# One level of Strassen's product in 12 of 22 blocks of an up projection, and a later split of the activations

## Chip, core and metric

The kernel runs on one core of a Trainium2 chip. The metric is the time of one execution on the device in microseconds (us); before the change it is 1796.58 us, the median of 3 runs (1796.41 to 1797.27). TensorE (PE) multiplies matrices and adds into PSUM; VectorE (DVE), ScalarE (ACT) and GpSimd (POOL) do everything else; SyncE (SP) issues most transfers from DRAM. Each engine works through its own instructions in order, and semaphores join them.

## What is computed

Two layers on a sequence of 512 tokens of width 1024, in float32: normalization and modulation, a projection for three attention-like branches, their gated merge, and a feed-forward part. The change concerns the last:

```python
h2 = modulate(rms_norm(x, norm2_g), shift2, scale2)
u, g = jnp.split(h2 @ w_up, 2, axis=-1)      # w_up: 1024 x 5632, u and g 2816 wide
u = causal_dwconv(u, w_conv, b_conv)         # 3 taps along the tokens
y = (jax.nn.silu(u) * g) @ w_down            # 2816 x 1024
x = x + gate2[:, None, :] * y
```

## The kernel before

Tokens lie along the free dimension (512 columns), features on the 128 partitions. To keep the precision of float32, each operand is split into a high part in the TensorE format float32r and a low part, the rest; a product takes three matmuls (mm3, L239): high weights by high activations (L240), high weights by low activations (L241), low weights by high activations (L242).

The weights lie in DRAM in the order of their use, as 302 units of 128 x 1024 (eight blocks of 128 x 128). Three engines handle each unit: SP loads it into one of 4 buffers wr (L113 to L115), ACT casts it to wh (L123), DVE subtracts to get wl (L132). prep_to and dma_to (called by ahead) keep these steps some units ahead of TensorE; there are 5 buffers each of wh and wl. A column block (col_block) is one unit: 24 matmuls of 512 columns into one PSUM bank. What evacuates the bank is appended to a list (pend) and emitted by flush within the next block, so the order of the instructions on DVE and ACT is that in which Python emits them; nothing reorders them.

The feed-forward part has 22 blocks j, each a column block for u and one for g. head_group makes the first three of each while the norm is still being finished. Then j = 3 to 21 follow one by one. ff_evac makes the convolution and Silu from PSUM (ACT L959, DVE L960 and L962, ACT L964), multiplies by g (DVE L965) and splits the result into fah (ACT L468) and fal (DVE L469), which the down projection reads: for each of 8 output blocks, 22 x 3 matmuls of 512 columns. Sums for adaLN (one load ar and one DVE instruction, L152, each) run along in every second tick. The activations x (8 tiles) stay in SBUF throughout; 60 slots of 128 x 512 serve all other tiles.

## Time and profile before

| | |
|---|---|
| median of 3 runs | 1796.58 us |
| the profiled execution | 1795.69 us, its span 1793.9 us |
| mean granted TensorE clock | 0.999 |
| moved by DMA | 220.00 MB, mean 123 GB/s |
| wh, 302 casts on ACT | 314.4 us busy |
| wl, 302 subtractions on DVE | 368.7 us busy |
| matmuls of L240, L241, L242 on hhi and hlo | 3 x 1296 |

Rows of groups read: line, engine, operation, output and inputs by the program's names, shape and count, then the busy time and the mean duration of one in ns, then idle time before them and what ended it. Rows of the timeline read: start in us, duration in us, engine, line, operation, and in brackets the idle time before it and what ended it. Matmuls overlap in their rows, so their pace is the distance between starts. Rows of windows read: the stretch, its length, busy time and count for PE, weight loads, DVE, ACT and POOL, then the granted clock (1.00 is full), the busy share of the DMA engines and GB/s.

### The profile page before, as it was taken

What the parts mean: (1) busy time and instruction counts of PE and PEld (TensorE: products, weight loads), DVE (VectorE), ACT (ScalarE), POOL (GpSimd) and SP (SyncE); (2) the same over time, 40 slices, a digit from 0 to 9 for tenths busy, and PEclk for the clock granted to TensorE, in tenths of its full rate; (3) what the DMA queues carried; (4) which work ended last, traced back from release to release, by engine and by line L of the source; (5) the groups of instructions that cost most, each with busy time, mean ns of one, the idle gap of its engine ahead of it and who ended that gap; (6) DMA issues with size and microseconds to landing.
All of it is one profiled execution on the core that took longest, in us unless ns stands there. A gap on an engine that the chain in (4) does not pass through costs nothing.

```text
span 1793.9 us, 22042 instructions
## 1 busy us (share of the span) xinstructions
PE 1781.2 (99%) x8737; PEld 1485.9 (83%) x8737; DVE 999.0 (56%) x1499; ACT 675.3 (38%) x1125; POOL 88.7 (5%) x112
## 2 busy tenths in 40 slices
PE   8999999999999999999999999999999999999999
PEld 6888778888888888888898887888888988888887
DVE  7777654565666876664256576534335465444321
ACT  4674433432324433332137543334223244333220
POOL 3221100000000000000002010000000000000000
PEclk9999999999999999999999999999999999999999
DMA  9332233455533565554223322322322223232231
GB/s 347 122 128 71 71 100 113 140 177 176 187 130 106 188 224 197 189 188 144 80 71 126 110 71 71 117 83 71 103 97 82 73 94 129 94 101 99 70 123 43
DMA packets 64947, 220.00 MB, mean 123 GB/s; under 512 B 7320, under 2 KB 7746, under 8 KB 64844
## 3 DMA queue, kind: packets, MB, share of 16 engines
q1 hardware_dynamic: 64140, 216.47, 36.0%
q0 software_dynamic: 704, 2.11, 0.4%
q8 instruction: 69, 1.13, 0.3%
q14 instruction: 34, 0.28, 0.0%
HBM read 216.44 MB, written 2.11 MB: 122 GB/s over the span
## 4 chain that ended last, share of the span: by engine, by line
PE 96%; DVE 3%; ACT 1%; DMA 0%; issue 0%; SPq 0%; POOL 0%; ACTq 0%; DVEq 0%
PE bm L240 24%; PE bm L242 24%; PE bm L241 24%; PE bm L369 4%; PE ga L369 4%; PE bm L537 3%; PE bm L538 3%; PE bm L539 3%; PE fs L654 1%; PE fo L680 1%; PE go L766 0%; DVE wl L132 0%; PE ro L821 0%; PE rs L794 0%; PE oT L753 0%; PE fT L670 0%
## 5 line engine op out<-in xcount | busy, mean ns | idle before, releaser
L132 DVE TENSOR_TENSOR wl<-wr,wh 128x1024 fp32r<-128x1024 f32 x302 | 368.7, 1224 | 317.5 <-ACT wh L123 317.0
L240 PE MATMUL bm<-hhi,wh 128*128 128x512 f32 x1296 | 515.7, 398 | 0.0
L242 PE MATMUL bm<-hhi,wl 128*128 128x512 f32 x1296 | 505.1, 390 | 0.0
L241 PE MATMUL bm<-hlo,wh 128*128 128x512 f32 x1296 | 504.8, 389 | 0.0
L123 ACT CAST wh<-wr 128x1024 fp32r<-128x1024 f32 x302 | 314.4, 1047 | 290.6 <-PE bm L241 218.3
L240 PEld LDWEIGHTS bm<-hhi,wh 128*128 128x128 f32 x1296 | 243.4, 188 | 52.1 <-issue 2.8
L242 PEld LDWEIGHTS bm<-hhi,wl 128*128 128x128 f32 x1296 | 243.2, 188 | 51.7
L241 PEld LDWEIGHTS bm<-hlo,wh 128*128 128x128 f32 x1296 | 243.5, 188 | 51.1 <-issue 1.4
L240 PE MATMUL bm<-fah,wh 128*128 128x512 f32 (+1 forms) x374 | 140.9, 377 | 0.0
L241 PE MATMUL bm<-fal,wh 128*128 128x512 f32 (+1 forms) x374 | 140.8, 377 | 0.0
L242 PE MATMUL bm<-fah,wl 128*128 128x512 f32 (+1 forms) x374 | 140.8, 377 | 0.0
L152 DVE SCALAR_TENSOR_TENSOR ar<-ar,cact 128x1024 f32<-128x1024 f32 x80 | 97.4, 1218 | 0.0
L537 PE MATMUL bm<-wh,hhi 128*128 128x512 f32 (+1 forms) x256 | 96.9, 379 | 0.0
L538 PE MATMUL bm<-wl,hhi 128*128 128x512 f32 (+1 forms) x256 | 93.5, 365 | 0.0
L539 PE MATMUL bm<-wh,hlo 128*128 128x512 f32 (+1 forms) x256 | 93.3, 365 | 0.0
L927 DVE SCALAR_TENSOR_TENSOR x<-bm,mod,x 128x512 f32<-128x512 f32 (+1 forms) x39 | 25.5, 654 | 100.0 <-PE bm L242 99.9
L240 PEld LDWEIGHTS bm<-fah,wh 128*128 128x128 f32 x374 | 70.4, 188 | 12.9
L241 PEld LDWEIGHTS bm<-fal,wh 128*128 128x128 f32 x374 | 70.4, 188 | 12.9
L242 PEld LDWEIGHTS bm<-fah,wl 128*128 128x128 f32 x374 | 70.4, 188 | 12.9
L965 DVE TENSOR_TENSOR fu<-fu,bm 128x512 f32<-128x512 f32 x42 | 28.9, 688 | 69.9 <-PE bm L242 61.6
L964 ACT ACTIVATE fu<-fu 128x512 f32<-128x512 f32 x44 | 27.8, 632 | 94.2 <-DVE fu L962 94.2
L890 ACT ACTIVATE mg<-bm,der 128x512 f32<-128x512 f32 x48 | 32.9, 685 | 73.7 <-PE bm L242 73.7
(230 smaller groups left out, 2346.5 us busy)
## 6 DMA issues: line engine op xcount, KB each, us to landing
wr<-wall SPq DMA_DIRECT2D x302, 512.0 KB, 3.4
ar<-wada SPq DMA_DIRECT2D x80, 512.0 KB, 3.3
ad<-wada SPq DMA_DIRECT2D x32, 256.0 KB, 6.3
x<-xT SPq DMA_DIRECT2D x8, 256.0 KB, 4.7
cumb<-cumd POOLq DMA_DIRECT2D x8, 256.0 KB, 4.7
dec<-tabs SPq DMA_DIRECT2D x8, 256.0 KB, 4.1
out<-x SPq DMA_DIRECT2D x8, 256.0 KB, 2.1
cos<-tabs SPq DMA_DIRECT2D x2, 256.0 KB
```

Source lines behind the costliest of these rows:

```text
L123: A.copy(hi, raw[i])
L132: V.tensor_tensor(lo, raw.pop(i), hi.bitcast(F32), op=ALU.subtract)
L152: V.scalar_tensor_tensor(out=r, in0=r, scalar=1.0, in1=cact, op0=ALU.mult, op1=ALU.mult, accum_out=mod[l][:, b:b + 1])
L240: T.matmul(o, lhsT=wh, rhs=ah, start=first, stop=False)
L241: T.matmul(o, lhsT=wh, rhs=al, start=False, stop=False)
L242: T.matmul(o, lhsT=wl, rhs=ah, start=False, stop=last)
L369: T.matmul(banks[f % GB][:, ts], lhsT=got[f // 8][wi][:, (f % 8) * 128:(f % 8) * 128 + 128], rhs=h[kc][hi][:, ts], start=kc == 0 and hf != ...
L537: T.matmul(o, lhsT=h[k][0][:, bs], rhs=wh[:, ws], start=k == 0, stop=False)
L538: T.matmul(o, lhsT=h[k][0][:, bs], rhs=wl[:, ws], start=False, stop=False)
L539: T.matmul(o, lhsT=h[k][1][:, bs], rhs=wh[:, ws], start=False, stop=k == KD - 1)
L890: A.activation(g, o, AF.Tanh, scale=0.5, bias=der[l][:, i * 8 + j:i * 8 + j + 1])
L965: V.tensor_tensor(t, t, pg, op=ALU.mult)
```

## The change

The last 12 blocks of each layer (j = 10 to 21) are made in three groups of four. In a group, the weights form a 2 x 2 matrix of halves: u and g by the first and second half of the 1024 inputs; the activations one of input halves by token halves. Seven products of halves take the place of eight. Each is 48 matmuls of 256 columns, in two units (the 14 of a group are called u0 to u13), and products that belong to one sum add up in PSUM or are added on evacuation.

- The sums of activations and their high and low parts (t_sum, t_low) are made once a layer, during j = 3 to 6.
- The sums of weights are made in the wr buffers by accumulating transfers of POOL (acc_to): 8 plain loads and 8 accumulating ones in a group. Cast and subtraction then run once for each of the 14 units, where 8 column blocks had 8.
- ff_conv reads its input from an SBUF tile (uu) in a group; e3 calls it twice for u10 and twice for u11; e4 multiplies by g after u12 and u13.
- The split into fah and fal is no longer made with each block but in the down projection (act_to), whose first two output blocks now run side by side over the 22 activations; the order of its weights follows (DN).
- x no longer stays in SBUF: it is stored to DRAM by POOL after the output projection (xm) and after the down projection (xs), and loaded again by SP where it is next needed. 56 slots remain.
- In the down projection the adaLN sums run in every tick (ada_fast); none run during the groups.

```diff
+def _plan():
+    v, w = [], [0]
+
+    def plain(n):
+        for _ in range(n):
+            v.append(("r", w[0], None))
+            w[0] += 1
+
+    def pair():
+        b = w[0]
+        a11, a21, a12, a22 = ((b + 2 * i, b + 2 * i + 1) for i in range(4))
+        for dst, src in ((a11, None), (a21, a22), (a12, None), (a21, a11), (a11, a21), (a21, a12), (a22, None)):
+            for i in range(2):
+                v.append(("r", dst[i], None if src is None else src[i]))
+        w[0] += 8
...
+    wr_p = ctx.enter_context(tc.tile_pool(name="wr", bufs=6))
+    uu_p = ctx.enter_context(tc.tile_pool(name="uu", bufs=4))
...
+    x = [slot("x") for _ in range(KD)]
...
+    def dma_to(u, soft=False):
+        while state["dma"] < wlim[min(u, NU)]:
             i = state["dma"]
+            if soft and sum(endv[k] >= state["lo"] for k in range(i)) >= 6:
+                return
             raw[i] = wr_p.tile([128, UW], F32, tag="wr", name="wr")
             Q.dma_start(out=raw[i], in_=wall[i])
             state["dma"] += 1
+
+    def acc_to(u):
+        while accs and accs[0][0] < u and accs[0][3] < state["lo"] and accs[0][1] in raw:
+            _, dst, src, _ = accs.pop(0)
+            G.dma_start(out=raw[dst], in_=wall[src], accum_op=ALU.add)
 
     def prep_hi(u):
         while state["prep"] < min(u, NU):
             i = state["prep"]
             dma_to(i + 1)
+            acc_to(i + 1)
             hi = wh_p.tile([128, UW], F32R, tag="wh", name="wh")
-            A.copy(hi, raw[i])
+            A.copy(hi, raw[plan[i][1]])
...
+            V.tensor_tensor(lo, raw[plan[i][1]], hi.bitcast(F32), op=ALU.subtract)
             wgt[i] = (hi, lo)
             state["lo"] += 1
+            acc_to(i + 6)
...
+        if ada_on[0] and (ada_fast[0] or tickcount[0] % 2 == 1):
...
+                for k in range(KD):
+                    x[k] = slot("x")
+                    Q.dma_start(out=x[k], in_=xT[k * 128:k * 128 + 128, :] if l == 0 else xs[k])
...
+        def upd(j, o, ts=FULL):
+            upd2(j, o, ts)
+            if (l, j) not in xm:
+                xm[l, j] = dr_p.tile([128, S], F32, tag=f"xm{j}", bufs=1, name="xm")
+            G.dma_start(out=xm[l, j][:, ts], in_=x[j][:, ts])
...
-            V.tensor_tensor(t, t, pg, op=ALU.mult)
-            act[j] = split(t, "fa")
+            act[j] = t
+
+        def ff_evac(j, pu, pg):
+            ff_conv(j, pu)
+            V.tensor_tensor(act[j], act[j], pg, op=ALU.mult)
...
+        def t_sum(k):
+            ta, tb = slot("ta"), slot("tb")
+            c, d = tks.pop((l, k)), tks.pop((l, k + 4))
+            V.tensor_tensor(ta[:, H0], c[:, H0], c[:, H1], op=ALU.subtract)
+            V.scalar_tensor_tensor(out=ta[:, H1], in0=d[:, H1], scalar=-1.0, in1=ta[:, H0], op0=ALU.mult,
+                                   op1=ALU.subtract)
+            V.scalar_tensor_tensor(out=tb[:, H0], in0=d[:, H1], scalar=tabd[:, k:k + 1], in1=c[:, H1], op0=ALU.add,
+                                   op1=ALU.subtract)
+            V.tensor_tensor(tb[:, H1], d[:, H1], d[:, H0], op=ALU.subtract)
+            V.tensor_tensor(tb[:, H1], tb[:, H1], ta[:, H0], op=ALU.add)
+            ah, bh = slot("tah", F32R), slot("tbh", F32R)
+            A.copy(ah[:, H0], ta[:, H0])
+            A.activation(ah[:, H1], ta[:, H1], AF.Identity, bias=tabd[:, 4 + k:5 + k])
+            A.copy(bh, tb)
...
+            al, bl = slot("tal", F32R), slot("tbl", F32R)
+            V.tensor_tensor(al[:, H0], ta[:, H0], ah[:, H0].bitcast(F32), op=ALU.subtract)
+            V.scalar_tensor_tensor(out=al[:, H1], in0=ta[:, H1], scalar=tabd[:, 4 + k:5 + k],
+                                   in1=ah[:, H1].bitcast(F32), op0=ALU.add, op1=ALU.subtract)
+            V.tensor_tensor(bl, tb, bh.bitcast(F32), op=ALU.subtract)
+            tt[k, 1], tt[k, 2] = (ah, al, 0), (ah, al, 256)
+            tt[k, 3], tt[k, 4] = (bh, bl, 0), (bh, bl, 256)
...
+        def ff_group(j0):
+            flush()
+            q = {}
+            for k in range(4):
+                q[k, 11], q[k, 12] = (*h2[k], 0), (*h2[k], 256)
+                q[k, 21], q[k, 22] = (*h2[k + 4], 0), (*h2[k + 4], 256)
+            bA, bB, bC = [bm(), bm()], [ba(), ba()], [bm(), ba()]
+            uu, gg = [None, None], [None, None]
+
+            def half(t, c):
+                return t.rearrange("p (a c b) -> p a c b", a=2, c=2)[:, :, c, :]
+
+            def bank(t):
+                return t.rearrange("p (a b) -> p a b", a=2)
+
+            def prod(banks, key, first, evac):
+                for t in range(2):
+                    flush()
+                    prep_lo(cur[0] + 3)
+                    prep_hi(cur[0] + 4)
+                    dma_to(cur[0] + 10, True)
+                    wh, wl = unit()
+                    for i in range(2):
+                        o = banks[t][:, i * 256:i * 256 + 256]
+                        for k in range(4):
+                            ah, al, c = q[k, key] if key > 4 else tt[k, key]
+                            sl = slice((i * 4 + k) * 128, (i * 4 + k) * 128 + 128)
+                            ah, al = ah[:, c:c + 256], al[:, c:c + 256]
+                            T.matmul(o, lhsT=wh[:, sl], rhs=ah, start=first and i == 0 and k == 0, stop=False,
+                                     skip_group_check=True)
+                            T.matmul(o, lhsT=wh[:, sl], rhs=al, start=False, stop=False, skip_group_check=True)
+                            T.matmul(o, lhsT=wl[:, sl], rhs=ah, start=False, stop=k == 3, skip_group_check=True)
+                    pend.append(lambda t=t: evac(t))
+
+            def e1(t):
+                uu[t] = uu_p.tile([128, 2 * S], F32, tag="uu", name="uu")
+                A.copy(half(uu[t], 0), bank(bA[t]))
+
+            def e5(t):
+                gg[t] = uu_p.tile([128, 2 * S], F32, tag="uu", name="gg")
+                A.copy(half(gg[t], 1), bank(bB[t]))
+
+            def e3(t):
+                V.tensor_tensor(half(uu[t], 1), half(uu[t], 1), bank(bB[t]), op=ALU.add)
+                for i in range(2):
+                    ff_conv(j0 + 2 * t + i, uu[t][:, i * S:i * S + S])
+
+            def e4(t):
+                A.activation(half(gg[t], 0), bank(bA[t]), AF.Copy, scale=-1.0)
+                for i in range(2):
+                    j = j0 + 2 * t + i
+                    V.tensor_tensor(act[j], act[j], gg[t][:, i * S:i * S + S], op=ALU.mult)
+
+            prod(bA, 11, True, e1)
+            prod(bB, 1, True, e5)
+            prod(bC, 21, True, lambda t: V.tensor_tensor(half(uu[t], 0), half(uu[t], 0), bank(bC[t]), op=ALU.add))
+            prod(bA, 2, False, lambda t: A.copy(half(uu[t], 1), bank(bA[t])))
+            prod(bA, 3, False, lambda t: V.scalar_tensor_tensor(out=half(gg[t], 1), in0=bank(bA[t]), scalar=-1.0,
+                                                                in1=half(gg[t], 1), op0=ALU.mult, op1=ALU.subtract))
+            prod(bB, 22, False, e3)
+            prod(bA, 4, False, e4)
+            free(3)
...
+            if TS:
...
+        far[0] = 3
+        for g in range(NG):
+            ff_group(J0 + 4 * g)
+        far[0] = 1
         flush()
         h2.clear()
-
-        upd5 = updater(5)
+        tt.clear()
+        for k in range(KD):
+            x[k] = slot("x")
+            Q.dma_start(out=x[k], in_=xm[l, k])
...
+        def act_to(n):
+            for k in range(min(n, KFF)):
+                if act[k] is None:
+                    act[k] = split(actf[k], "fa")
...
+                G.dma_start(out=xs[j][:, ts], in_=x[j][:, ts])
...
+        act_to(2)
+        o2 = [bm(), bm()]
+        for kc in range(KFF):
+            act_to(kc + 4)
+            for j in range(2):
+                wh, wl = wd(j, kc)
+                mm3(o2[j], wh, wl, act[kc][0], act[kc][1], kc == 0, kc == KFF - 1)
+            if kc % 2:
+                tick()
+        for j in range(2):
+            pend.append(lambda j=j: dn_evac(j, o2[j]))
...
-NSLOT = 60
+NSLOT = 56```

On DVE, at the end of a group, the order changes as follows. Before, the end of one block's work in the plain loop (wl: a unit's low weights; fu: the convolution; ar: an adaLN sum):

```order
L132 TENSOR_TENSOR wl_6239<-wr_6207,wh_6237 128x1024
L960 SCALAR_TENSOR_TENSOR fu_6256<-bm_6165,par0_82,fu_6256 128x511
L962 SCALAR_TENSOR_TENSOR fu_6256<-bm_6165,par0_82,fu_6256 128x510
L965 TENSOR_TENSOR fu_6256<-fu_6256,bm_6209 128x512
L469 TENSOR_TENSOR fal_6263<-fu_6256,fah_6262 128x512
L152 SCALAR_TENSOR_TENSOR ar_6235,mod1_85<-ar_6235,cact_90 128x1024
L132 TENSOR_TENSOR wl_6283<-wr_6241,wh_6281 128x1024
```

One convolution stood between the low weights of two units, each of which lasted a column block.

Now, from the end of u10 of the first group in layer 0 (ba_5535 and ba_5536 are the banks of u10 and u11; wl_5897 is the low part of u13, wl_5938 that of the next group's first unit, wl_5969 of its second):

```order
L1132 TENSOR_TENSOR uu_5570<-uu_5570,ba_5535 128x2x256
L1042 SCALAR_TENSOR_TENSOR fu_5887<-uu_5570,par0_85,fu_5887 128x511
L1044 SCALAR_TENSOR_TENSOR fu_5887<-uu_5570,par0_85,fu_5887 128x510
L1042 SCALAR_TENSOR_TENSOR fu_5892<-uu_5570,par0_85,fu_5892 128x511
L1044 SCALAR_TENSOR_TENSOR fu_5892<-uu_5570,par0_85,fu_5892 128x510
L188 TENSOR_TENSOR wl_5897<-wr_5673,wh_5858 128x1024
L1132 TENSOR_TENSOR uu_5603<-uu_5603,ba_5536 128x2x256
L1042 SCALAR_TENSOR_TENSOR fu_5928<-uu_5603,par0_85,fu_5928 128x511
L1044 SCALAR_TENSOR_TENSOR fu_5928<-uu_5603,par0_85,fu_5928 128x510
L1042 SCALAR_TENSOR_TENSOR fu_5933<-uu_5603,par0_85,fu_5933 128x511
L1044 SCALAR_TENSOR_TENSOR fu_5933<-uu_5603,par0_85,fu_5933 128x510
L188 TENSOR_TENSOR wl_5938<-wr_5734,wh_5899 128x1024
```

Two convolutions now stand ahead of each of two units' low weights. Behind these rows follow two products (L1140), wl_5969 and two more products.

On ACT, at the end of a layer's up projection, before (fah_6401 is the last block's split; the wh behind it belong to the down projection):

```order
L123 CAST wh_6359<-wr_6319 128x1024
L959 ACTIVATE fu_6395<-bm_6321,par0_82 128x512
L964 ACTIVATE fu_6395<-fu_6395 128x512
L468 CAST fah_6401<-fu_6395 128x512
L123 CAST wh_6407<-wr_6363 128x1024
L123 CAST wh_6440<-wr_6411 128x1024
```

Now, from the last group's u11 on (fu_6854 and fu_6859 are its two convolutions; bm_6464 and bm_6465 the banks of u12 and u13; fah_6947 is the high part of activation 0, with which the down projection begins):

```order
L1041 ACTIVATE fu_6854<-uu_6531,par0_85 128x512
L1046 ACTIVATE fu_6854<-fu_6854 128x512
L1041 ACTIVATE fu_6859<-uu_6531,par0_85 128x512
L1046 ACTIVATE fu_6859<-fu_6859 128x512
L179 CAST wh_6866<-wr_6693 128x1024
L1137 ACTIVATE gg_6562<-bm_6464 128x2x256
L179 CAST wh_6899<-wr_6724 128x1024
L1137 ACTIVATE gg_6594<-bm_6465 128x2x256
L538 CAST fah_6947<-fu_4943 128x512
L538 CAST fah_6951<-fu_4949 128x512
```

The first of the splits moved from the first blocks of the feed-forward part to behind the evacuation of the last unit; on DVE the first low part (fal_6948) likewise stands behind the last two products.

More of the change, by code (lines that the diff above doesn't have):

```diff
@@ L51 @@
 NC = _o
+NG = 3
+J0 = KFF - 4 * NG
+DN = [(j, k) for k in range(KFF) for j in range(2)] + [(j, k) for j in range(2, KD) for k in range(KFF)]
+DNI = {t: i for i, t in enumerate(DN)}
+H0 = slice(0, S // 2)
+H1 = slice(S // 2, S)
+def _plan():
[11 more added lines that the diff above has]
+        w[0] += 8
+    for _ in range(L):
+        plain(8 + 4 + 1 + 3 + 1 + 4 + 12 + 4 + 4 + 36 + 8 + 6 + 2 * (J0 - 3))
+        for _ in range(NG):
+            pair()
+        plain(KFF)
+    lim, m = [0], 0
+    for t in v:
+        m = max(m, t[1] + 1)
+        lim.append(m)
+    return v, lim
 @with_exitstack
@@ L104, in tile_hybrid_layers, with dbg @@
     warm = const.tile([128, S], BF16, tag="warm", name="warm")
-    x = [const.tile([128, S], F32, tag=f"x{k}", name=f"x{k}") for k in range(KD)]
+    x = [slot("x") for _ in range(KD)]
     state = {"prep": 0, "lo": 0, "dma": 0}
     raw, wgt = {}, {}
-    NU = wall.shape[0]
-    def dma_to(u):
-        while state["dma"] < min(u, NU):
+    plan, wlim = _plan()
+    NU = len(plan)
+    def dbg(*a):
+        if DBG:
+            print(*a, tickcount[0], "unit", cur[0])
+    endv, accs, last = {}, [], {}
+    for i, t in enumerate(plan):
+        if t[2] is not None:
+            accs.append((i, t[1], t[2], last.get(t[1], -1)))
+        endv[t[1]] = last[t[1]] = i
+    def dma_to(u, soft=False):
+        while state["dma"] < wlim[min(u, NU)]:
             i = state["dma"]
+            if soft and sum(endv[k] >= state["lo"] for k in range(i)) >= 6:
+                return
             raw[i] = wr_p.tile([128, UW], F32, tag="wr", name="wr")
@@ L225, in tick @@
         advance("p")
-        if ada_on[0] and tickcount[0] % 2 == 1:
+        if ada_on[0] and (ada_fast[0] or tickcount[0] % 2 == 1):
             ada_step()
         tickcount[0] += 1
+        if DBG:
+            print("T", tickcount[0], len(active), len(queue), live[0], cur[0], [g[0].__name__ for g in active])
     tickcount = [0]
@@ L232, in tile_hybrid_layers @@
     ada_on = [True]
+    ada_fast = [False]
     def drain():
@@ new lines, in layer @@
+        TS = [lambda: t_sum(0), lambda: t_low(0), lambda: t_sum(1), lambda: t_low(1),
+              lambda: t_sum(2), lambda: t_low(2), lambda: t_sum(3), lambda: t_low(3)]
+        def ff_group(j0):
[52 more added lines that the diff above has]
+            free(3)
@@ L972, in layer @@
         free(NA)
-        for j in range(3, KFF):
+        for j in range(3, J0):
             hold = {}
@@ L1002, in store, with dn_evac @@
             Q.dma_start(out=out[j * 128:j * 128 + 128, ts], in_=x[j][:, ts])
-        for j in range(KD if last else KD - 1):
+        def dn_evac(j, o):
+            upd5(j, o)
+            if last:
+                store(j)
+            else:
+                square_acc(j, acc3)
+        act_to(2)
[9 more added lines that the diff above has]
+            pend.append(lambda j=j: dn_evac(j, o2[j]))
+        for j in range(2, KD if last else KD - 1):
             o = bm()
```

68 lines of the change are left out of this document (52 added, 16 removed).

## The prediction

> **What bounds the kernel now.** I read the page first, then the waits of TensorE, then the timeline, one engine at a time.
>
> ```profile
> span 1793.9 us, 22042 instructions
> PE 1781.2 (99%) x8737; PEld 1485.9 (83%) x8737; DVE 999.0 (56%) x1499; ACT 675.3 (38%) x1125; POOL 88.7 (5%) x112
> PE 96%; DVE 3%; ACT 1%; DMA 0%; issue 0%; SPq 0%; POOL 0%; ACTq 0%; DVEq 0%
> PE fT L670 <- DVE st L738: 2.5, 2, 1.3
> PE nrm L293 <- DVE acc L278: 2.5, 1, 2.5
> ```
>
> TensorE is busy for 99% of the span and makes up 96% of the chain that ended last; its two longest waits are 2.5 us in all. So the kernel lasts as long as its matmuls follow each other, and a busy matmul row says little (it overlaps the next). What counts is the distance from one start to the next.
>
> ```profile
> 639.92 0.39 PE L240 MATMUL bm<-hhi,wh 128*128 128x512 f32 x1
> ...
> 652.16 0.39 PE L240 MATMUL bm<-hhi,wh 128*128 128x512 f32 x1
> ...
> 536.99 0.28 PE L240 MATMUL bm<-mxh,wh 128*128 128x256 f32 x1
> ...
> 541.18 0.28 PE L242 MATMUL bm<-mxh,wl 128*128 128x256 f32 x1
> ```
>
> Between the first two rows (feed-forward) lie 54 steps: 12.24 / 54 = 0.2267 us for 512 columns. Between the last two (256 columns, a new weight load before each) lie 35: 4.19 / 35 = 0.1197 us. A matmul of half the width costs 53% of a whole one.
>
> **Term 1, the matmuls.** A group of four feed-forward blocks took 8 column blocks of 24 matmuls, 8 x 24 x 0.2267 = 43.5 us. It becomes 7 products x 2 halves x 24 = 336 matmuls of 256 columns, 40.2 us. Three groups in each of two layers: 6 x (40.2 - 43.5) = **-19.8 us**, though 12.5% of the multiplications go. One half product (I call the 14 of a group u0 to u13) lasts 24 x 0.1197 = 2.87 us, where a column block lasted 5.44 us. So everything prepared once per unit has half the time.
>
> **Term 2, the ends of the groups.** e3 evacuates u10 and u11, each with an addition and two convolutions. Rows of before for such work:
>
> ```profile
> 641.05 0.39 PE L242 MATMUL bm<-hhi,wl 128*128 128x512 f32 x1
> 641.55 0.69 DVE L965 TENSOR_TENSOR fu<-fu,bm 128x512 f32<-128x512 f32 x1 [0.94 <-PE bm L242]
> 642.92 0.69 DVE L469 TENSOR_TENSOR fal<-fu,fah 128x512 fp32r<-128x512 f32 x1 [0.69 <-ACT fah L468]
> 643.53 1.22 DVE L152 SCALAR_TENSOR_TENSOR ar<-ar,cact 128x1024 f32<-128x1024 f32 x1
> ...
> 642.27 0.62 ACT L468 CAST fah<-fu 128x512 fp32r<-128x512 f32 x1 [0.94 <-DVE fu L965]
> 642.80 1.05 ACT L123 CAST wh<-wr 128x1024 fp32r<-128x1024 f32 x1
> ...
> 648.92 0.74 DVE L960 SCALAR_TENSOR_TENSOR fu<-bm,par,fu 128x511 f32<-128x511 f32 x1
> 649.70 0.75 DVE L962 SCALAR_TENSOR_TENSOR fu<-bm,par,fu 128x510 f32<-128x510 f32 x1
> ...
> 650.54 0.63 ACT L964 ACTIVATE fu<-fu 128x512 f32<-128x512 f32 x1 [2.12 <-DVE fu L962]
> ...
> L132 DVE TENSOR_TENSOR wl<-wr,wh 128x1024 fp32r<-128x1024 f32 x302 | 368.7, 1224 | 317.5 <-ACT wh L123 317.0
> L321 ACT ACTIVATE hhi<-ht,mod 128x512 fp32r<-128x512 f32 x23 | 16.7, 725 | 40.9 <-POOL mod L346 23.9 <-DVE ht L320 16.9
> L326 DVE SCALAR_TENSOR_TENSOR hlo<-ht,mod,hhi 128x512 fp32r<-128x512 f32 x23 | 17.2, 746 | 0.0
> L673 ACT COPY fpT<-fT 128x512 f32<-128x512 f32 x8 | 4.7, 585 | 4.7 <-PE fT L670 4.6
> ```
>
> They give the durations: 0.69 for an addition or product with PSUM, 0.75 for a scalar-tensor-tensor from SBUF (L326), 0.72 for an activation with a column as bias from SBUF (L321), 0.63 for Silu, 0.62 for a cast of 512, 0.60 for a copy from PSUM (near L673), 1.05 for wh, 1.22 for wl. And the hops: 0.03 to 0.09 from engine to engine; the next independent instruction starts 0.08 before the last one ends; DVE starts 0.5 after the start of a block's last matmul, so for 256 columns (0.11 shorter) 0.26 after the next unit could start.
>
> The order on DVE and ACT (shown with the change) puts e3 of u10, then the low weights of u13, then e3 of u11, then the low weights of the next group's first unit v0. Within e3 the two engines take turns: the second convolution's first activation stands behind the first one's Silu on ACT. With u10 starting at 0, TensorE wants u13 at 8.62 and v0 at 11.49, the low weights 0.24 later each (third matmul).
>
> - u10 ends 2.87; DVE adds 3.13 to 3.82; ACT 3.86 to 4.58; DVE 4.62 to 6.15; Silu 6.24 to 6.87, activation to 7.50; DVE 7.54 to 9.07; wl of u13 8.99 to **10.21**. Wanted at 8.86: TensorE waits 1.4.
> - The same for u11: addition 10.13 to 10.82, ACT to 11.58, DVE to 13.15, ACT to 14.50, DVE to 16.07, wl of v0 to **17.21**. u13 resumed at 10.3 and ends at 12.93, so v0 wants it at 13.17: 4.1 more.
> - Behind it on ACT: Silu 16.79, wh 17.75, copy of u12 18.26, wh 19.22, copy of u13 19.73. On DVE two products to 19.60, wl of v1 to 20.74, wanted at 20.17: 0.6. Then the queue is short again (v2's is done at 23.1, wanted at 23.7).
>
> So 6.2 us for each inner end, four of them: **+24.8 us**. At a layer's last group the down projection follows, whose first matmul needs the first activation's high part, which is now cast on ACT behind the copy of u13: 19.64 to 20.26. TensorE is free at 12.93 and starts at 20.35 (7.4), then waits for the low part, on DVE behind wl to 20.74 and two products to 21.96: 22.57, 2.1 more. With u13's 1.4 that is 10.9, twice: **+21.9 us**. Behind it, each step of two columns over one activation takes TensorE 6 x 0.2267 = 1.36; in layer 0 DVE needs 0.61 + 0.29 + 0.6 (low part, a quarter of wl, half an adaLN sum) = 1.5 for it, so at 22 steps up to 2 us more; I take 0, since it starts ahead by three activations.
>
> **Term 3, the clock.** A waiting TensorE can lose it, as at the start:
>
> ```profile
> 5.84 3.59 PE L1049 MATMUL warm<-warm 128*128 128x512 bf16 x8
> 11.96 1.05 PE L293 MATMUL nrm<-ones,acc 128*128 128x1 f32 x8 [2.53 <-DVE acc L278]
> ...
> 13.00:14.00 1.00, 1.00 (x5) 0.38 (x3) 0.21 (x3) 0.00 (x0) 0.71 (x1) 0.57 0.93 360
> 14.00:15.00 1.00, 1.00 (x5) 0.46 (x4) 0.56 (x5) 0.00 (x0) 0.30 (x1) 0.50 1.03 356
> 15.00:16.00 1.00, 1.00 (x7) 1.00 (x7) 0.97 (x5) 0.00 (x0) 0.00 (x0) 0.50 0.99 383
> 16.00:17.00 1.00, 1.00 (x6) 0.69 (x6) 0.93 (x5) 0.97 (x1) 0.00 (x0) 0.72 1.04 397
> ```
>
> After 2.53 us of nothing and 0.9 us of one-column matmuls, the granted clock (third number from the end) is 0.57, 0.50, 0.50, 0.72 for a microsecond each: 1.7 us of work lost. The two layer ends idle far longer: 2 x 1.7. The inner ends idle 4.1 at once; between no loss and all of it I take half, 4 x 0.85. Together **+6.8 us**. The Trainium skill, TensorE: Matmul & The Clock Gate, section Part 1, says that the clock halves after a whole idle window of about 3.4 us which runs free of the kernel; the rows above agree. By it a wait of 4.1 holds such a window in 0.7 of 3.4 cases, an estimate of 1.4 us for the inner ends instead of 3.4, and a sum 2 us lower.
>
> **What costs nothing, and behind what.**
>
> ```profile
> 641.28:652.16 10.88, 10.88 (x50) 9.01 (x48) 7.77 (x12) 3.99 (x6) 0.00 (x0) 1.00 0.70 252
> wr<-wall SPq DMA_DIRECT2D x302, 512.0 KB, 3.4
> cumb<-cumd POOLq DMA_DIRECT2D x8, 256.0 KB, 4.7
> ...
> L602 POOL DMA_DIRECT2D cumb<-cumd x8: 538/538/595, 124.5 to 1011.8; - x8
> DMA to landing us min/median/max: 3.7/4.7/6.3
> ...
> 22.00:30.00 8.00, 8.00 (x37) 6.64 (x36) 7.62 (x16) 3.45 (x4) 3.35 (x8) 1.00 1.04 409
> ...
> 531.99 0.48 DVE L927 SCALAR_TENSOR_TENSOR x<-bm,mod,x 128x256 f32<-128x256 f32 x1 [1.49 <-PE bm L242]
> ...
> 534.73 0.70 POOL L297 TENSOR_TENSOR r<-v,cst 128x2 f32<-128x2 f32 x1 [168.48 <-DVE v L296]
> ```
>
> The sums and low parts of the activations for four k (t_sum, t_low) put about 3.9 us more on DVE in each pair of column blocks of j = 3 to 6, less 0.6 for the split that left: 11.1 of 10.88 us, where 7.77 were busy. The low weights are queued three units ahead, so a backlog of some microseconds stays hidden, and j = 7 to 9 work it off; at worst 6 us a layer. The 36 extra units of wh and wl lie on engines with room outside the ends. x is reloaded from DRAM by SP long before it is used, into buffers freed long before. Its stores stand on POOL ahead of the norm's power (L297); one issue takes 0.54 us and the last is due at 532.5, the power at 534.73, so nothing; at worst 4 x 0.54.
>
> The accumulating loads are new: no row has one. A group needs 8 loads and 8 accumulations of 0.52 MB in 46 us, 180 GB/s, where 409 were reached. From below: a plain wr load takes 3.4 us. From above: twice the slowest of these transfers of POOL for twice the bytes, 12.6. Each is issued three or more units before its use; if they run one after another on POOL's queue, they bind from 46.4 / 8 = 5.8 us each. I take 0, near the load. The Trainium skill, DMA: Bandwidth & Descriptors, section Anatomy of one DMA, gives 2.0 us and 436 GB/s for a transfer of POOL: an estimate of 3.2 us, or 4.4 if the addend counts as a second transfer, both under 5.8. That lowers the chance of the second rival.
>
> **The sum.** -19.8 + 24.8 + 21.9 + 6.8 = +33.7. The profiled execution took 1795.7 us (its span and 1.8 around), 0.9 below the median of 1796.58; so 1796.6 + 33.7 = 1830 us.
>
> **The rivals.**
>
> - *The turns overlap* (faster). If ACT's work in e3 were hidden, DVE alone would need 2 x (0.69 + 4 x 0.75) + 2 x 1.22 = 9.8 from u10's end to wl of v0, a wait of 1.2 at an inner end; a layer's end would still cost copy, two products and the low part, 2.9. -19.8 + 4.8 + 5.8 = -9.2: 1787 us. For it speaks that DVE has work for 14 x 1.22 + 2 x (5 x 0.69 + 4 x 0.75) = 30 of a group's 40 us; against it the order of the rows. It decides where all waits and the lost clock are under 19.8, 37% of mine.
> - *The accumulations bind.* At 6.3 us each, 50.4 for a group instead of 46.4: 6 x 4 = +24, 1854 us; at 12.6 far over 2000. For: the queue of POOL is one; against: the 409 GB/s.
> - *Half the waits* (a lead in the low weights that I don't see): 1803 us, or the same as before if a little less.
>
> **Chances.** The waits as worked out 0.70, the accumulations 0.12, overlap 0.12, in between 0.06. A measurement of this kernel can tell 0.2%, 3.6 us. Faster 0.13, within 0.2% 0.04, slower 0.83. The range takes in the half of the waits and the accumulations at 6.3: 1801 to 1856.
>
> **What would show it.** On TensorE's waits: L1120 (the third matmul, for wl) with some 1.4, 4.1 and 0.6 at each group's end, the down projection's first matmul for ACT's cast with 7.4, the next for the low part with 2.1; a granted clock under 1 behind the layer ends alone or behind all six. TensorE's step of 0.12 within the groups shows term 1. I am wrong if those waits are short, if TensorE waits for wh behind an accumulating load, or if the step isn't 0.12.

## The result, and the profile after

The changed kernel takes 1848.61 us (median of four runs, 1844.73 to 1848.94) where the kernel before took 1796.49 us: a ratio of 1.0284, with a 95% interval of 1.0266 to 1.0302. It is slower by 2.8%. The forecast was 1830 us with a range of 1801 to 1856, so the median lies 18.6 us above it. The profiled execution is the quickest of the four, 1844.73 us, which is 49.0 us above that of before; the sums below are made against it. The other three took some 4 us more, at a mean granted clock of 0.987 or 0.988 where it had 0.990.

First the page of the changed kernel: the span, the busy time of the engines, the shares of the chain that ended last, and two groups of DMA issues (the last column is the median from issue to landing).

```profile
span 1842.8 us, 24293 instructions
PE 1781.7 (97%) x9601; PEld 1523.5 (83%) x9601; DVE 1087.2 (59%) x1639; ACT 743.1 (40%) x1233; POOL 147.1 (8%) x191
PE 72%; DVE 14%; ACT 6%; DMA 5%; issue 2%; POOL 0%; SPq 0%; ACTq 0%; POOLq 0%; DVEq 0%
wr<-wall SPq DMA_DIRECT2D x302, 512.0 KB, 3.7
wr<-wall POOLq DMA_DIRECT2D x48, 512.0 KB, 9.1
```

TensorE is as busy as before (1781.7 us against 1781.2) in a span 48.9 us longer. On the chain its share fell from 96% to 72%; DVE and ACT have 20% of it, and DMA 5%. Before, DMA had none. So the change didn't save busy time by this page (rows of half the width overlap less), and the end of the kernel is no longer set by matmuls alone.

Then TensorE's waits, summed by what ended them (in all, times, longest):

```profile
PE bm L1120 <- DVE wl L188: 24.1, 10, 4.0
PE bm L300 <- ACT fah L538: 14.4, 2, 7.2
PE bm L301 <- DVE fal L539: 3.1, 2, 1.5
...
PE bm L1117 <- ACT uu L1145: 2.3, 5, 0.8
...
PE ba L1117 <- ACT wh L179: 2.1, 1, 2.1
...
PE ba L1120 <- DVE wl L188: 0.8, 1, 0.8
```

The first three are the waits that were forecast; the other three are not. The timeline of TensorE says where they stand. These are all its waits of 0.2 us or more from the end of layer 0's first group to the first matmuls of its down projection:

```profile
698.69 0.38 PE L1120 MATMUL bm<-tbh,wl 128*128 128x256 f32 x1 [1.35 <-DVE wl L188]
705.84 0.39 PE L1120 MATMUL bm<-hhi,wl 128*128 128x256 f32 x1 [4.02 <-DVE wl L188]
730.60 0.39 PE L1117 MATMUL bm<-tbh,wh 128*128 128x256 f32 x1 [0.21 <-ACT uu L1145]
746.84 0.38 PE L1120 MATMUL bm<-tbh,wl 128*128 128x256 f32 x1 [1.35 <-DVE wl L188]
753.99 0.39 PE L1120 MATMUL bm<-hhi,wl 128*128 128x256 f32 x1 [4.02 <-DVE wl L188]
779.22 0.39 PE L1117 MATMUL bm<-tbh,wh 128*128 128x256 f32 x1 [0.69 <-ACT uu L1145]
795.45 0.38 PE L1120 MATMUL bm<-tbh,wl 128*128 128x256 f32 x1 [1.34 <-DVE wl L188]
805.56 0.79 PE L300 MATMUL bm<-fah,wh 128*128 128x512 f32 x1 [7.21 <-ACT fah L538]
807.89 0.79 PE L301 MATMUL bm<-fal,wh 128*128 128x512 f32 x1 [1.54 <-DVE fal L539]
```

At u13 TensorE waits 1.35 us, at the next group's first unit 4.02, at a layer's end 7.21 and 1.54: the forecast had 1.4, 4.1, 7.4 and 2.1. (Within the stream a row of 256 columns is 0.28 us long though the next could start after 0.12, so each wait costs about 0.16 us more than the number in its bracket.)

The granted clock is read from the windows view (third number from the end), here in stretches of 3.41 us:

```profile
662.72:666.13 3.41, 0.79 (x5) 0.38 (x3) 2.41 (x3) 2.05 (x3) 0.00 (x0) 1.00 1.00 271
666.13:669.54 3.41, 3.18 (x15) 3.19 (x16) 0.91 (x2) 1.82 (x3) 2.63 (x3) 0.50 0.76 195
700.27:703.68 3.41, 1.55 (x13) 1.35 (x12) 1.91 (x3) 1.33 (x2) 0.00 (x0) 1.00 0.55 179
703.68:707.09 3.41, 1.25 (x10) 1.25 (x11) 2.32 (x4) 2.35 (x4) 0.00 (x0) 1.00 0.00 0
707.09:710.50 3.41, 3.41 (x18) 3.41 (x17) 3.41 (x6) 2.62 (x5) 0.00 (x0) 0.50 0.00 0
...
751.47:754.88 3.41, 0.89 (x7) 0.89 (x8) 2.43 (x3) 1.99 (x4) 0.00 (x0) 1.00 0.00 0
```

Behind every one of the four inner ends, and behind the wait at the start of layer 0's first group, one such stretch runs at half clock; behind each layer's end it is three (10.24 us). The first number after the comma is TensorE's busy time: 0.79, 1.25 and 0.89 us ahead of a halved stretch (that behind the last row, at 754.88, is one too), 1.55 us ahead of one that isn't. Ahead of the two halved stretches at the inner ends of layer 1 (from 1615.04 and 1662.82) it was 0.00.

Last, one group's length of the chain (layer 1, from the wait for one group's first unit to that for the next):

```profile
1619.18 0.68 DVE fu L1140
1619.86 1.15 DVE wl L188
1621.04 0.48 issue
1621.53 0.85 POOL wr L171
1622.43 0.50 POOL wr L171
1622.96 0.54 POOL wr L171
1623.50 14.82 DMA wr<-wall
1638.42 1.05 ACT wh L179
1639.47 0.49 ACT uu L1145
1640.01 0.39 PE bm L1117
...
1648.95 0.70 DVE uu L1132
1649.67 0.82 ACT fu L1041
1650.52 0.76 DVE fu L1042
...
1655.06 1.14 DVE wl L188
```

TensorE is on this chain for 8.9 of 48 us, from 1640.0 to 1648.9. The rest is a **ring**: the products of e4 and the low weights of u2 and u3 on DVE; four accumulating loads (for u6 to u9) that POOL issues together once those low weights have freed the buffers, the last landing 14.82 us later; wh, and behind it on ACT the copy of u6; u8 to u10 on TensorE; e3 with its turns between DVE and ACT; and again low weights. Its length, not the matmuls', is the length of a group.

### The profile page after: what moved, and what is told of

Its sections match the earlier page's. It is cut to its first block, busy times and chain, and to the rows that moved or that the text cites. A ratio compares the mean times of both kernels' runs of the same rounds, so it can differ in the third digit from the quotient of the medians.

```text
span 1842.8 us, 24293 instructions
## 1 busy us (share of the span) xinstructions
PE 1781.7 (97%) x9601; PEld 1523.5 (83%) x9601; DVE 1087.2 (59%) x1639; ACT 743.1 (40%) x1233; POOL 147.1 (8%) x191
## 4 chain that ended last, share of the span: by engine, by line
PE 72%; DVE 14%; ACT 6%; DMA 5%; issue 2%; POOL 0%; SPq 0%; ACTq 0%; POOLq 0%; DVEq 0%
PE bm L301 16%; PE bm L300 16%; PE bm L302 16%; DMA wr<-wall 5%; PE bm L439 4%; PE ga L439 4%; PE bm L607 3%; PE bm L608 3%; PE bm L609 3%; DVE wl L188 2%; ACT wh L179 2%; DVE fu L1044 1%; DVE fu L1042 1%; DVE fl L731 1%; DVE ar L209 1%
## 5 line engine op out<-in xcount | busy, mean ns | idle before, releaser
L188 DVE TENSOR_TENSOR wl<-wr,wh 128x1024 fp32r<-128x1024 f32 x338 | 411.6, 1223 | 316.9 <-ACT wh L179 313.4
L179 ACT CAST wh<-wr 128x1024 fp32r<-128x1024 f32 x338 | 349.7, 1045 | 265.3 <-PE bm L301 126.0
L300 PE MATMUL bm<-hhi,wh 128*128 128x512 f32 x912 | 366.1, 401 | 0.0
L302 PE MATMUL bm<-hhi,wl 128*128 128x512 f32 x912 | 355.7, 390 | 0.0
L301 PE MATMUL bm<-hlo,wh 128*128 128x512 f32 x912 | 355.5, 390 | 0.0
L300 PEld LDWEIGHTS bm<-hhi,wh 128*128 128x128 f32 x912 | 171.4, 188 | 37.2 <-issue 2.8
L302 PEld LDWEIGHTS bm<-hhi,wl 128*128 128x128 f32 x912 | 171.2, 188 | 36.8
L301 PEld LDWEIGHTS bm<-hlo,wh 128*128 128x128 f32 x912 | 171.5, 188 | 35.8 <-issue 1.4
L300 PE MATMUL bm<-fah,wh 128*128 128x512 f32 (+1 forms) x374 | 143.1, 383 | 14.4 <-ACT fah L538 14.4
L301 PE MATMUL bm<-fal,wh 128*128 128x512 f32 (+1 forms) x374 | 143.3, 383 | 3.2 <-DVE fal L539 3.1
L302 PE MATMUL bm<-fah,wl 128*128 128x512 f32 (+1 forms) x374 | 142.6, 381 | 0.0
L300 PEld LDWEIGHTS bm<-fah,wh 128*128 128x128 f32 x374 | 71.6, 191 | 28.2 <-ACT fah L538 14.8
L301 PEld LDWEIGHTS bm<-fal,wh 128*128 128x128 f32 x374 | 71.4, 191 | 19.0 <-DVE fal L539 5.8
L302 PEld LDWEIGHTS bm<-fah,wl 128*128 128x128 f32 x374 | 71.4, 191 | 12.9
L171 POOL DMA_DIRECT2D wr<-wall x48 | 41.7, 989 | 406.7 <-DVE wl L188 143.6
L1046 ACT ACTIVATE fu<-fu 128x512 f32<-128x512 f32 x44 | 27.8, 631 | 100.2 <-DVE fu L1044 100.2
L1120 PE MATMUL bm<-tbh,wl 128*128 128x256 f32 x192 | 54.9, 286 | 8.1 <-DVE wl L188 8.1
## 6 DMA issues: line engine op xcount, KB each, us to landing
wr<-wall SPq DMA_DIRECT2D x302, 512.0 KB, 3.7
ar<-wada SPq DMA_DIRECT2D x80, 512.0 KB, 4.7
wr<-wall POOLq DMA_DIRECT2D x48, 512.0 KB, 9.1
```

The lines of the kernel that those rows point to most:

```text
L171: G.dma_start(out=raw[dst], in_=wall[src], accum_op=ALU.add)
L179: A.copy(hi, raw[plan[i][1]])
L188: V.tensor_tensor(lo, raw[plan[i][1]], hi.bitcast(F32), op=ALU.subtract)
L300: T.matmul(o, lhsT=wh, rhs=ah, start=first, stop=False)
L301: T.matmul(o, lhsT=wh, rhs=al, start=False, stop=False)
L302: T.matmul(o, lhsT=wl, rhs=ah, start=False, stop=last)
```

## The experiments

All are edits of the changed kernel. Each time is a median; the kernel before ran beside them, at 1796.5 to 1796.8 us.

**The turns.** In e3, the two convolutions of a half product side by side:

```diff
-                for i in range(2):
-                    ff_conv(j0 + 2 * t + i, uu[t][:, i * S:i * S + S])
+                ff_conv2(j0 + 2 * t, uu[t])
...
+            for d, nm in ((1, "cw1"), (2, "cw0")):
+                for i in range(2):
+                    V.scalar_tensor_tensor(out=tt2[i][:, d:S], in0=pu[i][:, 0:S - d], scalar=pp(l, nm, j + i),
+                                           in1=tt2[i][:, d:S], op0=ALU.mult, op1=ALU.add)
+            for i in range(2):
+                A.activation(tt2[i], tt2[i], AF.Silu)
```

> Edit: in e3 the two convolutions of one half product are written side by side (activation, activation, four scalar-tensor-tensors, Silu, Silu) instead of one behind the other; same instructions, nothing left out. Theory (turns: DVE and ACT wait for each other at the end of a group, 1.35 + 4.02 us at an inner end): the wait at u13 goes, that at the next group's first unit falls to about 2.2 us, the layer ends get some 2.9 us shorter, and some or all of the four halvings of the clock behind the inner ends (1.7 us each) go. So 17 to 24 us less: 1825 to 1832 us. Rival A (DVE has simply too much work there, the turns don't matter): under 5 us, 1844 to 1849. Rival B (the accumulating loads of POOL's queue set the pace): what is won at the ends is waited for behind the loads, under 8 us, 1841 to 1849.

Measured: 1826.18 us. From TensorE's timeline, two inner ends and a layer's end:

```profile
704.29 0.39 PE L1133 MATMUL bm<-hhi,wl 128*128 128x256 f32 x1 [2.10 <-DVE wl L188]
...
748.77 0.39 PE L1133 MATMUL bm<-hhi,wl 128*128 128x256 f32 x1 [2.10 <-DVE wl L188]
...
796.73 0.79 PE L300 MATMUL bm<-fah,wh 128*128 128x512 f32 x1 [5.30 <-ACT fah L538]
```

The same instructions in another order took 22.4 us less. The wait at u13 is gone, 4.02 became 2.10, and a group takes 44.48 us (704.29 to 748.77) instead of 48.15. The turns in e3 are a cause, as forecast. A part came back elsewhere: TensorE's waits for ACT's copy of u6 grew, in layer 0 from 0.21 and 0.69 us to 0.96 and 1.47.

**The convolutions later, and the first activations earlier.** Two edits, alone and together: e3's convolutions and e4's products go into a list, of which each following unit takes one piece behind its weight preparation; and four activations are split inside the layer's last group, one a unit behind product 2.

```diff
                     dma_to(cur[0] + 10, True)
+                    if late:
+                        late.pop(0)()
+                    if spl:
+                        spl.pop(0)()
                     wh, wl = unit()
...
-                    ff_conv(j0 + 2 * t + i, uu[t][:, i * S:i * S + S])
+                    late.append(lambda i=i: ff_conv(j0 + 2 * t + i, uu[t][:, i * S:i * S + S]))
```

> Edit: e3 only adds; its four convolutions and e4's products go into a list from which each following half product takes one piece, behind its weight preparation (so the last pieces fall into the next group's first two units). Nothing left out. Theory: the four inner ends' waits (4 x 5.37), their halvings (4 x 1.7), both waits at u13 of the last groups (2 x 1.35) and some 0.16 us of lost overlap at each of ten stalls go; the layer ends get shorter by some 1.5 us each, no more. Together some 35 us less: 1809 to 1818 us. Rival A (too much DVE work in a group's second half): waits move to the next group's units and a third or less is won, 1836 to 1848. Rival B (accumulating loads bind once TensorE comes earlier): 1825 to 1840, with TensorE waiting for wh or for the copies that stand behind wh.

> Edit: the first four activations are split into high and low part inside the last group of a layer, one a unit behind product 2 (whose operands' slots they take), instead of behind the group's last evacuations. Nothing left out. Theory: at both layer ends the waits of 7.21 and 1.54 us and the halved clock behind them (some 2.9 and 2.1 us) go, the four inner ends stay as they are: some 22 us less, 1824 to 1829 us. Rival (what comes behind on ACT and DVE, the products and low parts, is late anyway, and TensorE only waits at a later activation): 8 us or less won, 1840 to 1848.

> Edit: the spread of e3's and e4's work and the early split of four activations together. Nothing left out. Theory (the gains add): 1848.6 - 35 - 22 = about 1792, range 1786 to 1799, so at the time of the kernel before or a little under it. Rival (accumulating loads bind, or DVE's work in a group is too much): 1805 to 1830.

Measured: 1824.91, 1849.33 and 1820.52 us. All three theories missed. The waits were of the kind that the rivals named (in e2_spread rival B); in time only e4_both lies inside its rival's range, e2_spread 0.1 us under rival B's, and e3_early 1.3 us above its own: it won nothing. In e2_spread no wait is left at the inner ends, but TensorE's timeline has others:

```profile
667.07 0.38 PE L1120 MATMUL ba<-tah,wh 128*128 128x256 f32 x1 [4.02 <-ACT wh L179]
...
728.38 0.39 PE L1120 MATMUL bm<-tbh,wh 128*128 128x256 f32 x1 [2.83 <-ACT uu L1150]
...
773.14 0.38 PE L1120 MATMUL bm<-tbh,wh 128*128 128x256 f32 x1 [2.67 <-ACT uu L1150]
```

TensorE comes to u8 earlier, and the copy of u6, which stands behind a wh that waits for an accumulating load, isn't there yet. In e3_early the waits at a layer's end only moved (TensorE's timeline again):

```profile
799.80 0.58 PE L1123 MATMUL bm<-tbh,wl 128*128 128x256 f32 x1 [3.03 <-DVE wl L188]
...
808.72 0.50 PE L302 MATMUL bm<-fah,wl 128*128 128x512 f32 x1 [4.21 <-DVE wl L188]
...
825.26 0.79 PE L301 MATMUL bm<-fal,wh 128*128 128x512 f32 x1 [4.60 <-DVE fal L539]
```

The first activation is ready, but the low weights of the down projection's first unit stand behind e3 just as those of a group's first unit do (4.21 against 4.02), and with the four splits ahead of it u13 waits longer (3.03 against 1.34). A layer's end is late by its whole queue, not by the one instruction that TensorE waits for first.

**The accumulating loads left out** of e2_spread:

> Edit: as e2_spread, and the 48 accumulating loads are left out, so the accumulated half products use plain weights (that part of the products is not computed as the reference has it). Theory (in e2_spread TensorE waits for the accumulating loads, by way of wh and of the copies that stand behind wh on ACT: 4.0 + 0.8 us in layer 0's first group and 0.65 + 2.83 + 2.67 + 1.62 + 2.26 us later, with four halvings of the clock of 1.7 us behind them): these 14.8 us and about 6 us of clock go, the layer ends stay: 1800 to 1808 us, where e2_spread took 1824.9. Rival (the copies are late because of ACT's own work, not because of the loads): under 5 us, 1820 to 1825.

Measured: 1803.42 us, 21.5 less than e2_spread, as the theory had it; between the groups' start and the layer's end only one wait of 0.51 us is left. So these loads do bind once the other waits are gone.

**The waits filled**, to see what the halved clock costs: idle matmuls behind each group's last one.

```diff
             prod(bA, 4, False, e4)
+            for _ in range(16 if j0 + 4 < KFF else 28):
+                T.matmul(bC[0], lhsT=warm[:, 0:128], rhs=warm, start=True, stop=True)
```

> Edit: the changed kernel with idle matmuls (512 columns of zeros into a bank that has been read) behind a group's last one: 16 (3.6 us) at an inner end, 28 (6.3 us) at a layer's end. The work that is waited for is the same, so the waits only change their name. Theory (a wait also costs the clock behind it): the halvings behind the four inner ends (1.7 us each) and most of those behind the two layer ends (2.9 and 2.1 us) go, the one in layer 0's first group stays: 8 to 12 us less, 1836 to 1841 us. Rival (the halved clock costs nothing, as DVE's queue is what is late there, and TensorE would only wait later): 1846 to 1850 us.

Measured: 1847.34 us: the rival's range. The totals can't be compared to the microsecond, since TensorE waited 5.05 us for wh in layer 0's first group here and 2.09 in the changed kernel's profile; so a later group is compared. The halvings behind the four inner ends are gone, yet a group of layer 1 takes 48.40 us (1617.34 to 1665.74 in TensorE's timeline) against 48.17 with them (1615.23 to 1663.40):

```profile
1617.34 0.39 PE L1120 MATMUL bm<-hhi,wl 128*128 128x256 f32 x1 [0.55 <-DVE wl L188]
...
1642.35 0.39 PE L1117 MATMUL bm<-tbh,wh 128*128 128x256 f32 x1 [1.36 <-ACT uu L1145]
...
1665.74 0.39 PE L1120 MATMUL bm<-hhi,wl 128*128 128x256 f32 x1 [0.55 <-DVE wl L188]
```

The saved clock came back as a wait for the copy (1.36 us where the changed kernel has 0.32 in this group): the ring doesn't contain that stretch of TensorE's work, so its clock doesn't matter there. But the rival's reason (DVE late by itself) isn't the one; the chain of this run has the four loads in the same place, 15.06 us long.

**A first try at a better kernel**: e4_both, with late pieces also inside the down projection, and wh prepared three units ahead instead of four, so that the copies don't stand behind it.

```diff
-                    prep_lo(cur[0] + 3)
-                    prep_hi(cur[0] + 4)
+                    prep_to(cur[0] + 3)
```

> Edit: e4_both, with the last pieces of the group taken one a step inside the down projection instead of ahead of it, and the high weights prepared three units ahead instead of four in the groups, so that the copies no longer stand behind a wh that waits for an accumulating load. Nothing left out. Theory (waits are all that the change costs, and the matmuls won 19.8 us): of e4_both's 1820.5 us the layer ends (2 x 8.4 and some 3 us of clock each) and the waits for the copies (7.6 and two halvings) go: 1780 to 1790 us, below the kernel before (1796.6). Rival A (the accumulating loads bind in themselves: TensorE waits for wh or wl instead of for the copies): 1792 to 1805. Rival B (DVE's work in the last group and at the start of the down projection is too much): 1795 to 1815 with waits for the low parts.

Measured: 1832.95 us, worse than e4_both and above the ranges of the theory and of both rivals. Now wh itself is late (0.69 us at a unit, then 0.76 for wl, several times a group): Silu waits 2.08 us on ACT for DVE, and the next cast stands behind it. The layer ends still wait 7.57 and 3.14 us. A miss on both counts.

**The order of the accumulating loads.** They stood in the order of use: u8's and u9's, whose buffers (a11) are free once u0's and u1's low weights are made, waited behind u6's and u7's. Now each goes as soon as its buffer has been read, and acc_to is called for ten units ahead instead of six:

```diff
-        while accs and accs[0][0] < u and accs[0][3] < state["lo"] and accs[0][1] in raw:
-            _, dst, src, _ = accs.pop(0)
-            G.dma_start(out=raw[dst], in_=wall[src], accum_op=ALU.add)
+        for a in [a for a in accs if a[0] < u and a[3] < state["lo"] and a[1] in raw]:
+            accs.remove(a)
+            G.dma_start(out=raw[a[1]], in_=wall[a[2]], accum_op=ALU.add)
...
-            acc_to(i + 6)
+            acc_to(i + 10)
```

> Edit: e2_spread, and an accumulating load is issued as soon as the buffer that it adds to has been read, also ahead of others that wait (before, the queue kept the order of use, so four to six of them stood together behind the low weights of u2 and u3, though two could go before). Nothing left out. Theory (the burst binds: loads one behind the other on one queue, 2.8 to 4.8 us from landing to landing, not the sum of all): the waits for the copies (0.65 + 2.83 + 2.67 + 1.62 + 2.26 us) and three halvings behind them go, the start of layer 0's first group (4.8 us) and the layer ends stay: 1807 to 1815 us, where e2_spread took 1824.9 and the same without the loads 1803.4. Rival (eight such loads a group are too many at any order): 1820 to 1830.

> Edit: the reordered accumulating loads; e3's convolutions cut into pieces of which each following half product takes one (activation, the two scalar-tensor-tensors and Silu of one convolution no longer in one piece), also inside the down projection; and eight activations split inside the layer's last group, five in its first half, three behind product 2. Nothing left out. Theory (the matmuls won 19.8 us, the waits were all the cost): some 5 us of waits with their clock at the start of layer 0's first group and 0 to 4 us elsewhere stay: 1780 to 1790 us against 1796.6 before. Rival A (the engines' in-order queues are overfull in the last group, the layer ends stay at 5 us or more each): 1790 to 1805. Rival B (the accumulating loads bind at any order): 1800 to 1815.

Measured: 1821.36 and 1803.55 us; both above the theory's range. Their times lie in the ranges of rivals (the loads too many, or binding, at any order); but the waits for the copies are gone in both, so that reason is left for layer 0's first group alone. In e9_all the waits at the layer ends are gone too, but for 2.35 us in layer 0's down projection, and layer 1 has no wait for a group or a down projection at all. The rest of the miss is in one place, the first group of layer 0, which got worse (TensorE's timeline of e9_all):

```profile
665.48 0.58 PE L1139 MATMUL ba<-tah,wh 128*128 128x256 f32 x1 [4.86 <-ACT wh L179]
666.74 0.58 PE L1142 MATMUL ba<-tah,wl 128*128 128x256 f32 x1 [0.47 <-DVE wl L188]
...
678.89 0.58 PE L1139 MATMUL ba<-tah,wh 128*128 128x256 f32 x1 [7.25 <-ACT wh L179]
```

**Layer 0's first group.** The next layer's modulation is loaded in layer 0 alone, through the weights' buffers. e10_all stops it two blocks ahead of the groups, e12 four. e11 puts the reordered loads under the filled waits of e6.

```diff
+            if j == J0 - 2:
+                ada_on[0] = False
+                while ada_raw:
...
```

> Edit: e9_all, and in layer 0 the next layer's modulation sums (ar: 512 KB loads that take buffers of the weights, each summed on DVE) stop two blocks earlier, ahead of the groups, and go on after the first two columns of the down projection, there at every second step instead of every fourth. Nothing left out. Theory (layer 0's first group waits 4.86 + 0.47 + 7.25 + 0.46 us for its accumulating loads, since the plain loads they add to stand behind the modulation's loads for a buffer; layer 1, without these loads, waits for nothing): these 13 us, the two halvings behind them (6.8 and 10.2 us at half clock, some 8 us), and the 2.35 us in the down projection go: 1779 to 1787 us, below the kernel before (1796.5). Rival (the buffers are not what is short: POOL's queue or the loads' rate at that place): 1795 to 1804. Second rival (the sums, put off, make DVE late in the down projection): 1786 to 1796, with waits for the low parts there.

> Edit: e6_filled_waits with the reordered accumulating loads of e8 and the earlier end of the modulation sums in layer 0 of e10. Nothing left out. Theory (in e6 the saved clock came back as waiting, since the period of a group, 48.2 us in the changed kernel, is set by a ring that TensorE's clock is not part of: low weights of u2 and u3, four loads one behind the other, wh, the copy of u6, u8, and from there e3 and the next group's low weights): without the burst the waits for the copies (1.36, 0.85, 1.36, 1.4 us) go and a group takes 40.2 + 5.4 + under 1.2 = 46 to 47 us in layer 1, where e6 has 48.5; with the start of layer 0's first group, 1826 to 1834 us, where e6 took 1847.3. Rival (the clock costs nothing for another reason, DVE's queue being late by itself): the groups of layer 1 stay at 48 us or more, 1836 to 1842.

> Edit: e10_all_ada, but the modulation sums of layer 0 stop four blocks ahead of the groups instead of two, and go on from the start of the down projection, at every fourth step for its first two columns and then at every second. Nothing left out. Theory (in layer 0 the weights are loaded too late by the modulation's loads, which stand between them for a buffer: the first accumulating load goes out 5 us ahead of the first group there, 18 us ahead in layer 1, where nothing waits): the lead grows, and the waits of layer 0's first group (1.24 + 0.76 + 5.08 + 0.46 us) and the halvings behind them (3.4 and 6.8 us at half clock, 5 us) go: 1779 to 1785 us, where e10 took 1792.5. Rival (the loads are late in layer 0 for another reason): 1789 to 1794. Second rival (42 sums in the down projection are more than DVE can hide there): 1784 to 1796, with waits for low parts or low weights in the down projection.

Measured: 1792.50 us (ratio to the kernel before 0.9977, 0.9966 to 0.9987), 1845.41 us, and 1787.73 us (0.9952, 0.9939 to 0.9966).

e10's and e12's theory came true in part: layer 0's first group waited 13.0 us in e9, 7.5 in e10 and 4.7 in e12, but not zero, so both times are above what was expected. Their second rivals' ranges take in both times, but the waits for low parts in the down projection that these rivals named didn't come. Nor is the theory's reason (the plain loads wait for a buffer) what helped in e10: the first accumulating load goes out when it did in e9 (649.28 against 649.16 us), and the first three land sooner, after 5.7, 7.5 and 9.5 us instead of 8.3, 9.0 and 12.3. In e9 two loads of SP go out beside them (at 650.03 and 655.20), in e10 none; that fits e10's first rival (the loads' rate at that place) better, though no run tries it alone. In e12 the first goes out earlier, at 643.64: 15.2 us ahead of the group's third unit, where layer 1 has 23.7. In e11 the part that the run was for came out: from 1618.48 to 1665.28, a group of layer 1 takes 46.8 us, inside the 46 to 47 expected, where e6 took 48.4. That TensorE's clock counts again with the burst out of the ring is argued, not shown: no run has the reordered loads and the halved clock at the inner ends together. The total missed its 1826 to 1834 by 11 us. It counted on a clean first group in layer 0, which waited 8.4 us in all (6.43 at its second accumulated unit) and lost some clock behind that.

e12 beats both kernels, the one before by 0.5%. Its page of waits, the three largest on TensorE (the last two are in the kernel before too), and then, from the view of line L171, its accumulating loads from issue to landing (in the changed kernel 5.3, 9.1 and 15.3):

```profile
PE ba L1139 <- ACT wh L179: 4.2, 1, 4.2
PE fT L741 <- DVE st L809: 2.5, 2, 1.3
PE nrm L355 <- DVE acc L340: 2.4, 1, 2.4
...
DMA to landing us min/median/max: 5.3/6.7/8.7
```

In its layer 1 the up projection goes from 1434.07 to 1660.43 on TensorE, 226.36 us, against 235.98 before (1433.94 to 1669.92): 9.6 us less for three groups, without a wait.

## Why the forecast was right in sign and short by 15 to 19 us

Point by point, on the profiled execution (+48.9 us of span):

| term | forecast | measured | from |
|---|---|---|---|
| matmuls | -19.8 | -19.8 | 24 steps of 256 columns in 2.87 us; e12's layer 1: -9.6 of -9.9 |
| four inner ends | +24.8 | +22.8 | 4 x (1.35 + 4.02 + 2 x 0.16) |
| two layer ends | +21.9 | +21.2 | 2 x (1.35 + 7.21 + 1.54 + 3 x 0.16) |
| clock | +6.8 | +13.4 | 5 x 1.7, and 2.8 and 2.1 behind the layer ends, by the granted clock |
| accumulating loads | 0 | +6.3 | 2.09 + 0.76 + 2.34, and 0.16 for each of seven waits |
| elsewhere | 0 | +2.9 | start 1.2; 0.9 in each layer's attention |

Together 46.8 of 48.9; 1.2 of the rest lies in layer 0's down projection, for which the forecast had up to 2 and took 0. The clock's row is some 1.5 us too large: TensorE's steps of 256 columns are 0.213 us apart at half clock (15 from 707.16 to 710.36) and 0.120 at full, so a halved stretch costs them 1.5 us, not 1.7.

- **The matmuls** did what was worked out: in e12 a group without waits takes 40.32 us in both layers (746.92 less 706.60, 1625.87 less 1585.55), where 40.2 was forecast and 43.5 taken before. The whole 19.8 us wasn't reached in any run, since layer 0's first group always waited.
- **The waits at the groups' ends** are where the forecast put them and nearly as long; only the 0.6 us at v1 didn't come. e1_turns shows that the order on DVE and ACT makes more than half of the wait at an inner end. That the sum came out so near is in part luck: the forecast let the matmuls pace a group between its ends, and in the trace a burst of 14.82 us stands there, which happens to end only 0.2 to 0.8 us after TensorE wants what hangs on it.
- **The step that failed in size is the clock.** I took half of the loss for an inner end. All four lost it, and so did the start of layer 0's first group, after a wait of 2.09 us. The rule that I weighed there, from the Trainium skill, TensorE: Matmul & The Clock Gate, section Part 1 (a halving needs a whole idle window of about 3.4 us), would have made it less; the trace disagrees: the stretches ahead of three halvings had 0.79, 1.25 and 0.89 us of matmuls in them. Of the inner ends only the two of layer 1 had a whole idle one. The rows at the start, which I held for agreement, had 1.05 us of one-column matmuls in that stretch too. As a cause the term is weaker than as a sum, though: e6 shows that the four inner halvings (6.8 us) were hidden behind the ring, and without them TensorE would have waited for the copies.
- **The loads that I took at nothing** were wrongly priced, and the sign that I named for it (TensorE waits for wh behind one of them) came, with 2.09 us. I bounded one by 12.6 us and let them bind from 5.8 us each, as if evenly spread. The quickest of the 48 takes 5.3 us, so the estimates of 3.2 and 4.4 were low; issued four at a time they land 2.8 to 4.9 us after each other, the last up to 15.3 us after its issue. In the changed kernel that costs only 6.3 us outright, since the waits at the groups' ends give the queue time. But the rival "the accumulations bind" was half true underneath: take the ends away (e2_spread) and they cost 21.5 us (e5). It isn't the queue's rate that binds, as that rival had it (from the first to the fourth landing in a burst are 3 x 3.8 us, so eight need 31 of a group's 40); it is the burst, and reordering it was enough everywhere but in layer 0's first group.
- **What was cheap as forecast**: the sums and low parts of the activations, the spill and the reload of x show no wait of TensorE.
- **Open**: the 0.9 us in each layer's attention (a wait of 0.57 us for ACT's copy L744, which all variants have, where the kernel before waits 0.2) was not tried; why the first accumulating load of layer 0 goes out with less lead than that of layer 1, in e12 too, neither. The 1.2 us at the start may not be the change's: the wait for the first norm is 1.7 to 3.4 us in the variants, none of which touches it.

## What to carry to other kernels

When a step makes TensorE's units half as long, everything done once per unit gets half the time; draw the queues of DVE and ACT behind the first late instruction before pricing a wait, and spread evacuations over the next units, one piece each. Follow the chain for a whole period of the loop: if it closes into a ring that TensorE is on for a fifth of the time, curing one wait turns it into the next. Ask of new transfers not only their rate but when their buffers come free, since loads that are all released by one instruction queue up.

## What the runs showed of the hardware

- The granted clock changes in stretches of 3.41 us. A stretch at half clock followed each one in which TensorE was busy for 1.25 us or less in the rows above (37%), and none followed 1.55 us (45%). The border isn't sharp: in other runs a halved stretch followed 1.68 us (e4_both, from 768.43) and 1.96 us (e7_best, from 754.67). Whole idleness isn't needed: in e1_turns a wait of 2.10 us was enough at 1603.20 and 1647.76, while the same wait at 704.29 and 748.77 had no halved stretch behind it; where a wait lies in the stretches decides.
- An accumulating load of 512 KB on POOL's queue takes 5.3 us at the quickest, against a median of 3.7 for the plain load on SP's queue, and such loads pass one after another: four issued within 2 us landed 5.3, 9.3, 12.5 and 14.8 us after their own issue (layer 1, second group).
